# Six orders of products and shifted weight blocks in a two-layer encoder

## Chip, cores and metric

The kernel runs on one core of a Trainium2 chip. The metric is the device time of one execution in microseconds. All inputs and outputs are float32 in HBM.

## What is computed

Two layers of an encoder over 272 tokens (256 and 16 learned ones) of 2048 features. Cut to what matters:

```python
def _layer(h, w_in, ..., w_out, ln1_w, ln1_b, w_ff1, w_ff2, ln2_w, ln2_b):
    proj = jnp.einsum('bld,dp->blp', h, w_in)          # 2048 -> 6176
    y_gla = _gla_mixer(...)                            # gated linear attention, 4 heads
    y_na = _na_mixer(...)                              # neighbourhood attention, 16 heads
    mix = jnp.einsum('blm,md->bld', jnp.concatenate([y_gla, y_na], axis=-1), w_out)
    h = _layer_norm(DEEPNORM_ALPHA * h + mix, ln1_w, ln1_b)
    ff = jnp.einsum('blf,fd->bld', jnp.square(jax.nn.relu(jnp.einsum('bld,df->blf', h, w_ff1))), w_ff2)
    return _layer_norm(DEEPNORM_ALPHA * h + ff, ln2_w, ln2_b)
```

Nearly all of the arithmetic is in the four weight products: w_in, w_out (2048 x 2048), w_ff1 (2048 x 8192) and w_ff2 (8192 x 2048).

## The kernel before, in words

**Products in halves.** TensorE multiplies in a reduced float32 format here, so each operand is split in a high part (a cast) and a low part (the operand less its high part). A product of a weight block W and activations X is then three: high W by high X (called **h** below), high W by low X (**l**), and low W by high X (**w**).

**Weight tiles.** Weights come from HBM as 768 tiles of 128 x 1024, that is eight blocks of 128 x 128 side by side. `made` (L172) issues the transfer into `raw` (L179), ScalarE casts it to `wh` (L180) and VectorE subtracts to `wl` (L181). The pool of these tiles has three buffers for each of raw, wh and wl, and `weights` (L166) makes tiles two ahead of the one in use. `head` (L186) does the same in pieces for the first tile, which arrives together with the first activations. A block of a tile starts 512 bytes after the one before it, in the high and in the low tile, and all these tiles start at multiples of 256 bytes in SBUF.

**Activations.** `pair` (L277) holds the high and low part of 128 features in one tile; a row has a pitch of 288 elements, so the low part lies 1152 bytes behind the high one and the next feature block 2304 bytes behind the first. Some pairs of the second layer are dense (256 and 256 elements).

**Two ways through a tile.** `by_m` (L250) takes one output of 128 features after the other; for each it calls `eight` (L204) once per weight tile, and all products of a call add up in one PSUM bank. `eight` writes out the order: for each of the eight blocks h and then l (L216), then for each of the eight blocks w (L219), so 24 products of up to 274 columns. Where only 256 tokens are needed it takes `once`: high and low activations as one moving operand of 512 columns (L213), eight products, and then eight w products of 256 columns into the second half of the bank (L219), 16 in all. `by_k` (L230) keeps four or eight outputs open at once and has an order of its own (L246).

**Around it.** Between calls `by_m` runs steps of the attention and norm work (`pump`, L121): small products on TensorE, vector work on ScalarE and VectorE. Evictions of finished outputs, casts and subtractions stand in the same queues of ScalarE and VectorE. All weight transfers are issued from SyncE's queue. The place of instructions in each queue is set by a scheduler at build time.

Of the kernel before, what the change touches and what calls it, by code (L numbers as in the profile page):

```python
# [7 lines left out]
F32 = mybir.dt.float32  # L8
F32R = mybir.dt.float32r
U8 = mybir.dt.uint8  # L10
AF = mybir.ActivationFunctionType
ALU = mybir.AluOpType
PSUM = bass.MemoryType.PSUM

P = 128
D = 2048
DC = D // P
T = 256
# [8 lines left out]
WB = 1024  # L27
# [10 lines left out]
MEET = 2  # L38
PAD = 40
PITCH = 288  # L40


class Pair(tuple):
# [10 lines left out]
class Trunk:  # L54
    def __init__(self, ctx, tc, ins, out):
        self.ctx, self.tc, self.nc = ctx, tc, tc.nc
        self.i, self.out = ins, out
        self.bg, self.fg, self.credit, self.fcredit = deque(), deque(), 0, 0
        self.wants, self.due, self.late = {}, None, 0
        self.x = [None] * DC  # L60
        self.stream, self.ready = self.order(), deque()
        pool = lambda name, **k: ctx.enter_context(tc.tile_pool(name=name, **k))
        self.cp = pool("const", bufs=1)
        self.xp = pool("xhl", bufs=1)
        self.yp = pool("yhl", bufs=1)
        self.wp = pool("wst", bufs=3)
        self.jp = pool("jn", bufs=1)
        self.pm = pool("pm", bufs=4, space=PSUM)
        self.pb = pool("pb", bufs=4, space=PSUM)
# [96 lines left out]
    def weights(self):  # L166

        while len(self.ready) < 2:
            self.ready.append(self.made(*next(self.stream, (None, ()))))
        return self.ready.popleft()  # L170

    def made(self, ap, ends):  # L172
        if ap is None:
            return None
        nc = self.nc
        raw, wh, wl = (self.wp.tile([P, WB], d, name=nm, tag=nm)
                       for nm, d in (("raw", F32), ("wh", F32R), ("wl", F32R)))
        for c in map(slice, (0,) + ends, ends):
            nc.sync.dma_start(raw[:, c], ap[:, c])  # L179
            nc.scalar.copy(wh[:, c], raw[:, c])  # L180
            self.wl = nc.vector.tensor_tensor(wl[:, c], raw[:, c], wh[:, c].bitcast(F32), ALU.subtract).ins  # L181
        if not ends:
            self.head(ap, raw, wh, wl)
        return wh, wl

    def head(self, ap, raw, wh, wl):  # L186

        nc, q = self.nc, WB // 4
        both = self.xr.tile([P, 2, q + L], F32, name="head", tag="head", bufs=1)
        self.x[:2] = [self.pair(self.xp, "x", c) for c in range(2)]  # L190
        for c in range(2):
            nc.sync.dma_start(both[:, c], self.i["head"][:, c])
        nc.sync.dma_start(raw[:, 2 * q:], ap[:, 2 * q:])
        for c in range(2):
            at = slice(c * q, c * q + q)
            h, lo = (t[:, :L] for t in self.x[c])
            todo = [(both[:, c, q:], h, lo), (both[:, c, :q], wh[:, at], wl[:, at])]
            for args in todo[::-1] if c else todo:
                self.split(*args)
        for at in (slice(2 * q, 3 * q), slice(3 * q, WB)):  # L200
            nc.scalar.copy(wh[:, at], raw[:, at])
            self.wl = nc.vector.tensor_tensor(wl[:, at], raw[:, at], wh[:, at].bitcast(F32), ALU.subtract).ins

    def eight(self, ps, wh, wl, x, n, first, last, once):  # L204

        mm = self.nc.tensor.matmul
        c = lambda w, j: w[:, j * P:j * P + P]  # L210
        for j, v in enumerate(x):
            if once:
                mm(ps, lhsT=c(wh, j), rhs=v.once, start=first and not j, stop=False)  # L213
                continue
            for i in range(2):
                mm(ps[:, :n], lhsT=c(wh, j), rhs=v[i][:, :n], start=first and not i + j, stop=False)  # L216
        o = ps[:, T:] if once else ps[:, :n]
        for j, (h, _) in enumerate(x):
            mm(o, lhsT=c(wl, j), rhs=h[:, :T if once else n], start=False, stop=last and j == 7)  # L219

    def whole(self, parts):

# [7 lines left out]
    def by_k(self, acts, n, before, wide=False):  # L230

        ps = [self.pm.tile([P, 512], F32, name="mm", tag="mm") for _ in range(4)]
        if wide:
            ps += [self.bank() for _ in range(4)]
        nk = len(acts)
        for k in range(0, nk, 2):
            before(k)
            for g in range(0, len(ps), 4):
                wh, wl = self.weights()
                parts = ((wh, 0), (wh, 1), (wl, 0))  # L240
                order = [(j, p, m) for j in range(2) for p in range(3) for m in range(4)]
                by_output = k == nk - 2 or k == 0 and not wide
                order.sort(key=lambda o: (o[0], o[2] // 2) if wide and not k + g else (by_output and o[2], o[1] // 2))
                for j, p, m in order:
                    c = j * 512 + m * P
                    self.nc.tensor.matmul(ps[g + m][:, :n], lhsT=parts[p][0][:, c:c + P], rhs=acts[k + j][parts[p][1]][:, :n],  # L246
                                          start=k + j + p == 0, stop=k == nk - 2 and j + p == 3)
        return [p[:, :n] for p in ps]

# [27 lines left out]
    def pair(self, pool, name, c):  # L277
        both = pool.tile([P, 2, PITCH], F32R, name=f"{name}{c}", tag=f"{name}{c}", bufs=1)
        return Pair(both, dense=name in ("y", "u") and not self.full)
# [94 lines left out]
    def load_gates(self):  # L374

        place = lambda c: self.yp.tile([P, 2, PITCH], F32, name=f"gw{c}", tag=f"y{c}", bufs=1).rearrange("p a c -> p (a c)")[:, :512]
        *self.wup, self.wlr = (place(c) for c in (8, 9, 10))
# [563 lines left out]
    def reuse(self, name, c, dtype):  # L941

        t = self.xp.tile([P, 2, PITCH], dtype, name=f"{name}{c}", tag=f"x{c}", bufs=1)
        return t.rearrange("p a c -> p (a c)")[:, :512]
# [235 lines left out]
```

## Time and profile before

| | |
|---|---|
| time, median of 3 runs (lowest to highest) | 2366.43 us (2366.19 to 2366.48) |
| the profiled execution's own time | 2366.29 us |
| its span, first to last instruction | 2364.5 us |
| mean granted TensorE clock | 0.999 |
| products of `eight` and `by_k` in the busy table | L216, L219, L213, L246 |
| HBM traffic over the span | 176 GB/s |

The page of the profile gives busy time by engine, the span in 40 slices, DMA queues, the chain of work that ended last, and groups of instructions. A group's line reads: source line, engine, operation, output and inputs by name, shapes, count; then busy time and the mean duration of one in ns; then idle time of the engine just before them and what ended it. PE stands for TensorE's products, PEld for its weight loads, which overlap them; DVE is VectorE, ACT is ScalarE. In the timeline a row merges a run of like instructions: start in us, extent in us, engine, line, names, shapes, and the number merged. A product's shape is rows x columns of the weight block and then the moving operand.

### The profile page before, as it was taken

Reading aid. Unit: us, or ns where it says so; the run is one execution under the profiler, and the core shown is the slowest. Engines: PE = TensorE matmul, PEld = TensorE weight load, DVE = VectorE, ACT = ScalarE, POOL = GpSimd, SP = SyncE. Lnnn points to the kernel's source line nnn. Section 1 sums busy time; section 2 is a strip of 40 time slices with the busy share of each in tenths; the row PEclk is TensorE's granted clock in tenths of the full one; section 3 lists DMA queues with packets and bytes.
Section 4 is the critical chain, followed back from the end, with each engine's and each line's share of the span. In section 5 each row is a group of like instructions: output and inputs, shape, how many; then the busy total and the mean of one; then the engine's idle time right before and its main releaser. Section 6 shows DMA issues by size and latency. Waiting matters only on the chain.

```text
span 2364.5 us, 44607 instructions
## 1 busy us (share of the span) xinstructions
PE 2356.2 (100%) x18180; PEld 2241.9 (95%) x18180; DVE 1520.8 (64%) x2432; ACT 1219.3 (52%) x2100; POOL 136.2 (6%) x200
## 2 busy tenths in 40 slices
PE   9999999999999999999999999999999999999998
PEld 9999999999999999999999899999988888888888
DVE  5588777775544455546576787778766455666654
ACT  5666664564433344444456666655644333444443
POOL 0021100100000000000030111101100000000000
PEclk9999999999999999999999999999999999999999
DMA  7454445555555555555555555455566666556664
GB/s 261 153 160 153 156 135 176 173 176 178 177 178 176 176 177 179 177 177 174 177 184 171 164 160 165 155 160 188 187 192 190 189 187 188 188 190 212 195 188 144
DMA packets 118301, 419.02 MB, mean 177 GB/s; under 512 B 13512, under 2 KB 14024, under 8 KB 118096
## 3 DMA queue, kind: packets, MB, share of 16 engines
q1 hardware_dynamic: 117808, 415.65, 55.8%
q8 instruction: 142, 2.33, 0.4%
q14 instruction: 63, 0.52, 0.1%
q10 hardware_dynamic: 288, 0.52, 0.1%
HBM read 414.03 MB, written 2.10 MB: 176 GB/s over the span
## 4 chain that ended last, share of the span: by engine, by line
PE 98%; DVE 1%; issue 0%; ACT 0%; POOL 0%; DVEq 0%; ACTq 0%; POOLq 0%
PE mm L216 35%; PE mm L219 29%; PE mm L213 22%; PE mm L246 6%; PE bg L246 1%; PE bg L757 1%; PE mm L696 1%; PE bg L557 0%; PE bg L403 0%; DVE wl L181 0%; PE mm L722 0%; PE mm L446 0%; PE bg L883 0%; PE bg L608 0%; PE bg L638 0%
## 5 line engine op out<-in xcount | busy, mean ns | idle before, releaser
L181 DVE TENSOR_TENSOR wl<-raw,wh 128x1024 fp32r<-128x1024 f32 (+1 forms) x768 | 941.8, 1227 | 621.5 <-ACT wh L180 618.4
L180 ACT CAST wh<-raw 128x1024 fp32r<-128x1024 f32 (+1 forms) x768 | 803.5, 1047 | 919.4 <-PE mm L216 367.7
L216 PE MATMUL mm<-x,wh 128*128 128x272 f32 (+2 forms) x4224 | 569.8, 287 | 0.0
L216 PEld LDWEIGHTS mm<-x,wh 128*128 128x128 f32 x4224 | 541.1, 188 | 0.8 <-PE mm L696 0.2
L219 PE MATMUL mm<-x,wl 128*128 128x272 f32 (+3 forms) x3264 | 466.9, 285 | 0.0
L219 PEld LDWEIGHTS mm<-x,wl 128*128 128x128 f32 x3264 | 437.5, 189 | 11.6
L213 PE MATMUL mm<-x,wh 128*128 128x512 f32 x1152 | 290.1, 394 | 0.0
L213 PEld LDWEIGHTS mm<-x,wh 128*128 128x128 f32 x1152 | 207.2, 189 | 37.9 <-PE mm L696 0.4
L219 PE MATMUL mm<-y,wl 128*128 128x272 f32 (+1 forms) x1408 | 200.5, 285 | 0.0
L219 PEld LDWEIGHTS mm<-y,wl 128*128 128x128 f32 x1408 | 189.5, 189 | 6.5
L216 PE MATMUL mm<-y,wh 128*128 128x272 f32 (+1 forms) x1440 | 193.3, 286 | 0.0
L216 PEld LDWEIGHTS mm<-y,wh 128*128 128x128 f32 x1440 | 184.3, 188 | 0.0
L213 PE MATMUL mm<-y,wh 128*128 128x512 f32 x688 | 172.6, 392 | 0.0
L219 PE MATMUL mm<-u,wl 128*128 128x272 f32 (+1 forms) x1024 | 145.8, 285 | 0.0
L213 PEld LDWEIGHTS mm<-y,wh 128*128 128x128 f32 x688 | 123.6, 189 | 21.9
L219 PEld LDWEIGHTS mm<-u,wl 128*128 128x128 f32 x1024 | 137.8, 189 | 4.8
L216 PE MATMUL mm<-u,wh 128*128 128x272 f32 (+1 forms) x1056 | 141.2, 286 | 0.0
L216 PEld LDWEIGHTS mm<-u,wh 128*128 128x128 f32 x1056 | 134.9, 188 | 0.0
L213 PE MATMUL mm<-u,wh 128*128 128x512 f32 x496 | 124.2, 392 | 0.0
L213 PEld LDWEIGHTS mm<-u,wh 128*128 128x128 f32 x496 | 89.2, 189 | 15.9
L246 PE MATMUL mm<-x,wh 128*128 128x272 f32 (+1 forms) x512 | 73.3, 288 | 0.0
L246 PEld LDWEIGHTS mm<-x,wh 128*128 128x128 f32 x512 | 67.9, 191 | 0.0
(273 smaller groups left out, 1856.5 us busy)
## 6 DMA issues: line engine op xcount, KB each, us to landing
raw<-in_wff SPq DMA_DIRECT2D x512, 512.0 KB, 3.6
raw<-in_win SPq DMA_DIRECT2D x190, 512.0 KB, 3.8
raw<-in_wout SPq DMA_DIRECT2D x64, 512.0 KB, 3.6
nb<-in_nab SPq DMA_DIRECT2D x16, 352.0 KB, 4.7
xraw<-in_xT SPq DMA_DIRECT2D x7, 272.0 KB, 5.2
out<-out SPq DMA_DIRECT2D x5, 256.0 KB, 3.2
brow<-in_norm SPq DMA_DIRECT2D x4, 256.0 KB, 4.8
gw<-in_wup SPq DMA_DIRECT2D x4, 196.0 KB
```

The lines of the kernel that those rows point to most:

```text
L180: nc.scalar.copy(wh[:, c], raw[:, c])
L181: self.wl = nc.vector.tensor_tensor(wl[:, c], raw[:, c], wh[:, c].bitcast(F32), ALU.subtract).ins
L213: mm(ps, lhsT=c(wh, j), rhs=v.once, start=first and not j, stop=False)
L216: mm(ps[:, :n], lhsT=c(wh, j), rhs=v[i][:, :n], start=first and not i + j, stop=False)
L219: mm(o, lhsT=c(wl, j), rhs=h[:, :T if once else n], start=False, stop=last and j == 7)
L246: self.nc.tensor.matmul(ps[g + m][:, :n], lhsT=parts[p][0][:, c:c + P], rhs=acts[k + j][parts[p][1]][:, :n], start=k + j + p == 0, stop=k ...
L696: nc.tensor.matmul(ps[hh][:, t * NKEY:t * NKEY + NKEY], lhsT=q[hs, NM + t * P:NM + t * P + P], rhs=k[hs, t, :], start=True, stop=True)
L757: nc.tensor.matmul(po[t][hs, :P], lhsT=v2[ts, hs] if rest else v1[:, t, hs], rhs=p2[ts, hh, :] if rest else p1[:, 2 * hh + t, :], start=re ...
```

## The change

Each pair of consecutive weight tiles draws four things from a fixed hash of its number: the step between blocks of the high tile, the step between blocks of the low tile (128 elements and 0, 16, 32 or 48 more), the offset of the first low block (0, 16, 32 or 48 elements), and one of six orders of the products of a call. In an order each letter is the next product of its kind; where the moving operand is 512 wide, the letters l are left out. The tiles grow from 1024 to 1472 elements, and the space comes from a scratch area for DMA descriptors, which is cut from 8192 to 2048 bytes per partition. `by_k` draws steps and offset too, and keeps its order. The cast and the subtraction now write eight blocks with a step.

```diff
+SKEWS = (0, 16, 32, 48)
+TURNS = ("hlhlhlhlhlhlhlhl wwwwwwww", "hlw hlw hlw hlw hlw hlw hlw hlw", "hlhlww hlhlww hlhlww hlhlww",
+         "hhhhhhhh llllllll wwwwwwww", "hhll hhll hhll hhll wwwwwwww", "hlhlhlhlwwww hlhlhlhlwwww")
+SPAN = 1472
...
-        raw, wh, wl = (self.wp.tile([P, WB], d, name=nm, tag=nm)
-                       for nm, d in (("raw", F32), ("wh", F32R), ("wl", F32R)))
+        raw = self.wp.tile([P, WB], F32, name="raw", tag="raw")
+        blocks = raw.rearrange("p (b c) -> p b c", c=P)
+        a, b, base, turn = self.draw()
+        wh, wl = self.skewed("wh", a, 0), self.skewed("wl", b, base)
         for c in map(slice, (0,) + ends, ends):
             nc.sync.dma_start(raw[:, c], ap[:, c])
-            nc.scalar.copy(wh[:, c], raw[:, c])
-            self.wl = nc.vector.tensor_tensor(wl[:, c], raw[:, c], wh[:, c].bitcast(F32), ALU.subtract).ins
+            self.halves(blocks, wh, wl, slice(c.start // P, c.stop // P))
...
+    def draw(self):
+
+        r = self.tiles // 2 * 2654435761 % 2 ** 32 >> 12
+        self.tiles += 1
+        return SKEWS[r % 4], SKEWS[r // 4 % 4], SKEWS[r // 16 % 4], TURNS[r // 64 % len(TURNS)]
+
+    def skewed(self, name, skew, base):
+        flat = self.wp.tile([P, SPAN], F32R, name=name, tag=name)
+        return bass.AP(flat.tensor, flat.offset + base, [flat.ap[0], [P + skew, WB // P], [1, P]])
+
+    def halves(self, raw, wh, wl, at):
+        self.nc.scalar.copy(wh[:, at], raw[:, at])
+        self.wl = self.nc.vector.tensor_tensor(wl[:, at], raw[:, at], wh[:, at].bitcast(F32), ALU.subtract).ins
...
-        c = lambda w, j: w[:, j * P:j * P + P]
-        for j, v in enumerate(x):
+        c = lambda w, j: w[:, j]
+        seen = dict.fromkeys("hlw", 0)
+        todo = [k for k in self.turn if k in ("hw" if once else "hlw")]
+        for i, kind in enumerate(todo):
+            j = seen[kind]
+            seen[kind] += 1
+            w, v, o = wl if kind == "w" else wh, x[j], ps[:, :n]
+            rhs = v[kind == "l"][:, :n]
             if once:
-                mm(ps, lhsT=c(wh, j), rhs=v.once, start=first and not j, stop=False)
-                continue
-            for i in range(2):
-                mm(ps[:, :n], lhsT=c(wh, j), rhs=v[i][:, :n], start=first and not i + j, stop=False)
-        o = ps[:, T:] if once else ps[:, :n]
-        for j, (h, _) in enumerate(x):
-            mm(o, lhsT=c(wl, j), rhs=h[:, :T if once else n], start=False, stop=last and j == 7)
+                rhs, o = (v.once, ps) if kind == "h" else (v[0][:, :T], ps[:, T:])
+            mm(o, lhsT=c(w, j), rhs=rhs, start=first and not i, stop=last and i == len(todo) - 1)
...
-    nc = bacc.Bacc("TRN2", target_bir_lowering=False, num_devices=1, dynamic_dma_scratch_size=8192)
+    nc = bacc.Bacc("TRN2", target_bir_lowering=False, num_devices=1, dynamic_dma_scratch_size=2048)
```

More of the change, by code (lines that the diff above doesn't have):

```diff
@@ L60, in __init__ @@
         self.x = [None] * DC
-        self.stream, self.ready = self.order(), deque()
+        self.stream, self.ready, self.tiles, self.turns = self.order(), deque(), 0, deque()
         pool = lambda name, **k: ctx.enter_context(tc.tile_pool(name=name, **k))
@@ L169, in weights @@
             self.ready.append(self.made(*next(self.stream, (None, ()))))
+        self.turn = self.turns.popleft()
         return self.ready.popleft()
@@ L173, in made, with head @@
         if ap is None:
+            self.turns.append(None)
             return None
         nc = self.nc
-        raw, wh, wl = (self.wp.tile([P, WB], d, name=nm, tag=nm)
-                       for nm, d in (("raw", F32), ("wh", F32R), ("wl", F32R)))
+        raw = self.wp.tile([P, WB], F32, name="raw", tag="raw")
+        blocks = raw.rearrange("p (b c) -> p b c", c=P)
+        a, b, base, turn = self.draw()
+        wh, wl = self.skewed("wh", a, 0), self.skewed("wl", b, base)
         for c in map(slice, (0,) + ends, ends):
             nc.sync.dma_start(raw[:, c], ap[:, c])
-            nc.scalar.copy(wh[:, c], raw[:, c])
-            self.wl = nc.vector.tensor_tensor(wl[:, c], raw[:, c], wh[:, c].bitcast(F32), ALU.subtract).ins
+            self.halves(blocks, wh, wl, slice(c.start // P, c.stop // P))
         if not ends:
-            self.head(ap, raw, wh, wl)
+            self.head(ap, raw, blocks, wh, wl)
+        self.turns.append(turn)
         return wh, wl
-    def head(self, ap, raw, wh, wl):
+    def draw(self):
[8 more added lines that the diff above has]
+        self.wl = self.nc.vector.tensor_tensor(wl[:, at], raw[:, at], wh[:, at].bitcast(F32), ALU.subtract).ins
+    def head(self, ap, raw, blocks, wh, wl):
         nc, q = self.nc, WB // 4
@@ L194, in head @@
         for c in range(2):
-            at = slice(c * q, c * q + q)
+            at = slice(2 * c, 2 * c + 2)
             h, lo = (t[:, :L] for t in self.x[c])
-            todo = [(both[:, c, q:], h, lo), (both[:, c, :q], wh[:, at], wl[:, at])]
+            todo = [(both[:, c, q:], h, lo), (both[:, c, :q].rearrange("p (b c) -> p b c", c=P), wh[:, at], wl[:, at])]
             for args in todo[::-1] if c else todo:
                 self.split(*args)
-        for at in (slice(2 * q, 3 * q), slice(3 * q, WB)):
-            nc.scalar.copy(wh[:, at], raw[:, at])
-            self.wl = nc.vector.tensor_tensor(wl[:, at], raw[:, at], wh[:, at].bitcast(F32), ALU.subtract).ins
+        for at in (slice(4, 6), slice(6, 8)):
+            self.halves(blocks, wh, wl, at)
     def eight(self, ps, wh, wl, x, n, first, last, once):
         mm = self.nc.tensor.matmul
-        c = lambda w, j: w[:, j * P:j * P + P]
-        for j, v in enumerate(x):
-            if once:
-                mm(ps, lhsT=c(wh, j), rhs=v.once, start=first and not j, stop=False)
-                continue
-            for i in range(2):
-                mm(ps[:, :n], lhsT=c(wh, j), rhs=v[i][:, :n], start=first and not i + j, stop=False)
-        o = ps[:, T:] if once else ps[:, :n]
-        for j, (h, _) in enumerate(x):
-            mm(o, lhsT=c(wl, j), rhs=h[:, :T if once else n], start=False, stop=last and j == 7)
+        c = lambda w, j: w[:, j]
[6 more added lines that the diff above has]
+            rhs = v[kind == "l"][:, :n]
+            if once:
+                rhs, o = (v.once, ps) if kind == "h" else (v[0][:, :T], ps[:, T:])
+            mm(o, lhsT=c(w, j), rhs=rhs, start=first and not i, stop=last and i == len(todo) - 1)
     def whole(self, parts):
@@ L244, in by_k @@
                 for j, p, m in order:
-                    c = j * 512 + m * P
-                    self.nc.tensor.matmul(ps[g + m][:, :n], lhsT=parts[p][0][:, c:c + P], rhs=acts[k + j][parts[p][1]][:, :n],
+                    self.nc.tensor.matmul(ps[g + m][:, :n], lhsT=parts[p][0][:, 4 * j + m], rhs=acts[k + j][parts[p][1]][:, :n],
                                           start=k + j + p == 0, stop=k == nk - 2 and j + p == 3)
```

## The prediction

> **What bounds the kernel now.** I read the page first: the busy line of each engine, the row of the granted clock, then the shares of the chain that ended last.
>
> ```profile
> span 2364.5 us, 44607 instructions
> ...
> PE 2356.2 (100%) x18180; PEld 2241.9 (95%) x18180; DVE 1520.8 (64%) x2432; ACT 1219.3 (52%) x2100; POOL 136.2 (6%) x200
> ...
> PEclk9999999999999999999999999999999999999999
> ...
> PE 98%; DVE 1%; issue 0%; ACT 0%; POOL 0%; DVEq 0%; ACTq 0%; POOLq 0%
> ```
>
> TensorE never waits, its clock is never throttled, and 98% of the chain is its own work. So the time is the sum of the steps from one product to the next, and an edit that leaves the number of products alone can act in two ways only: by the length of a step, or by making TensorE wait where it does not wait today. The groups give the counts, and the two costly feeders:
>
> ```profile
> L181 DVE TENSOR_TENSOR wl<-raw,wh 128x1024 fp32r<-128x1024 f32 (+1 forms) x768 | 941.8, 1227 | 621.5 <-ACT wh L180 618.4
> L180 ACT CAST wh<-raw 128x1024 fp32r<-128x1024 f32 (+1 forms) x768 | 803.5, 1047 | 919.4 <-PE mm L216 367.7
> L216 PE MATMUL mm<-x,wh 128*128 128x272 f32 (+2 forms) x4224 | 569.8, 287 | 0.0
> ...
> L213 PE MATMUL mm<-x,wh 128*128 128x512 f32 x1152 | 290.1, 394 | 0.0
> ...
> L216 PE MATMUL mm<-y,wh 128*128 128x272 f32 (+1 forms) x1440 | 193.3, 286 | 0.0
> L213 PE MATMUL mm<-y,wh 128*128 128x512 f32 x688 | 172.6, 392 | 0.0
> ...
> L216 PE MATMUL mm<-u,wh 128*128 128x272 f32 (+1 forms) x1056 | 141.2, 286 | 0.0
> ...
> L213 PE MATMUL mm<-u,wh 128*128 128x512 f32 x496 | 124.2, 392 | 0.0
> ```
>
> The mean of one (287 ns) is a latency; neighbours overlap, so it is not the price of a product. L216 issues 16 products a tile: 4224 + 1440 + 1056 = 6720, that is 420 **narrow tiles** of 24 products (nearly all 272 wide). L213 issues 8: 1152 + 688 + 496 = 2336, that is 292 **wide tiles** of eight 512-wide and eight 256-wide products. The price is in TensorE's timeline, from one row's start to the next. First narrow tiles, then (two further windows that cut into the run at 401.70) single products, then a wide tile and its second half:
>
> ```profile
> 399.72 2.14 PE L216 MATMUL mm<-y,wh 128*128 128x272 f32 x16
> 401.70 1.16 PE L219 MATMUL mm<-y,wl 128*128 128x272 f32 x8
> 402.70 2.14 PE L216 MATMUL mm<-y,wh 128*128 128x272 f32 x16
> 404.68 1.16 PE L219 MATMUL mm<-y,wl 128*128 128x272 f32 x8
> 405.68 0.54 PE L216 MATMUL mm<-y,wh 128*128 128x272 f32 x3
> ```
>
> ```profile
> 401.82 1.04 PE L219 MATMUL mm<-y,wl 128*128 128x272 f32 x7
> ```
>
> ```profile
> 401.95 0.91 PE L219 MATMUL mm<-y,wl 128*128 128x272 f32 x6
> ```
>
> ```profile
> 1900.92 2.00 PE L213 MATMUL mm<-u,wh 128*128 128x512 f32 x8
> 1902.76 1.12 PE L219 MATMUL mm<-u,wl 128*128 128x256 f32 x8
> 1903.71 2.00 PE L213 MATMUL mm<-y,wh 128*128 128x512 f32 x8
> ```
>
> ```profile
> 1901.85 1.07 PE L213 MATMUL mm<-u,wh 128*128 128x512 f32 x4
> ```
>
> A narrow tile takes 402.70 - 399.72 = 2.98 us, 124.2 ns a product: 123.8 in the high run, 125.0 in the low run. Within one run the steps differ: 0.12 us from 401.70, then 0.13 us, and the six that follow take 0.75 us (125). A wide tile takes 2.79 us; its 512-wide run starts slowly (four in 0.93 us, 232.5 ns each) and settles (four in 0.91 us, 227.5 each); its 256-wide run takes 0.95 us, 118.8 each. So a product of the same width has no fixed price; something in its place and its neighbours moves it by some per cent, and that is what the change shuffles.
>
> **The change part by part.** Products, loads of weights, casts, subtractions and transfers are as many as before; the two built programs hold the same instructions on every engine, with some casts, subtractions and small vector operations changing places. What remains are five edits.
>
> *Order and steps of blocks, narrow tiles.* No row shows narrow tiles with blocks apart by 576, 640 or 704 bytes. The nearest rows are the products of L246: same width, same tiles, another order and another place for the output. The chain in order of time gives whole stages of them, each piece from its first start to the next piece's:
>
> ```profile
> 357.26 15.23 PE mm L246 x120
> ...
> 493.82 24.10 PE mm L246 x192
> ...
> 1679.72 23.04 PE mm L246 x192
> ```
>
> 192 products of 272 columns in 24.10 us are 125.5 ns each; the 120 at 357.26 took 126.9. The 256-wide ones at 1679.72 took 120.0 each, the lowest that a long run shows. So the ends are 120 (-4.2 ns) and 130 (+5.8, the worst step above), that is -42 and +58 us over 420 x 24 products. I take the nearest row: +1.3 ns, 24 x 1.3 = 0.031 us a tile, **+13.0 us** over 420 tiles. I apply it to all six orders, the first (today's) too, since it also gets new steps.
>
> *Steps of blocks, wide tiles.* The nearest row is a wide tile whose moving operand lies in two pieces, in another place to its weights:
>
> ```profile
> 1499.69 2.02 PE L213 MATMUL mm<-x,wh 128*128 128x512 f32 x8
> 1501.55 1.11 PE L219 MATMUL mm<-x,wl 128*128 128x256 f32 x8
> 1502.49 2.17 PE L216 MATMUL mm<-x,wh 128*128 128x272 f32 x16
> ```
>
> Its 512-wide run takes 1.86 us and does not settle (232.5 each); the tile takes 2.80 us instead of 2.79. Ends: 227.5 and 232.5 in all eight instead of 230, -0.02 and +0.02 us a tile. I take +0.01 x 292 = **+2.9 us**.
>
> *Order, wide tiles.* L213's tiles have no l products. Three of the six orders are then today's (144 of the 292 tiles). The order hlw becomes hw eight times (52 tiles): at the settled prices 8 x (227.5 + 118.8) = 2.77 us, -0.02 each, **-1.0 us**. hlhlww and the two half runs (96 tiles) start a high run again and again: 8 x (232.5 + 118.8) = 2.81 us, +0.02 each, **+1.9 us**.
>
> *Stepped writes of the cast and the subtraction.* The trace has such writes: ws, 512 elements in 16 blocks, beside the plain 512-element cast of L180 (the 620 in the row of all casts).
>
> ```profile
> L268 ACT CAST ws<-gw x2: 622/622/623, 27.6 to 1253.9; 128x512 fp32r<-128x512 f32 x2
> L269 DVE TENSOR_TENSOR ws<-gw,ws x2: 686/686/687, 39.1 to 1260.8; 128x512 fp32r<-128x512 f32 x2
> ```
>
> ```profile
> L180 ACT CAST wh<-raw x768: 620/1048/1062, 6.8 to 2341.9; 128x1024 fp32r<-128x1024 f32 x191, 128x512 fp32r<-128x512 f32 x1
> ```
>
> 622 against 620 ns: I count nothing; bounds 0 and 2 ns x 768 on engines that are 52 and 64% busy.
>
> *Later release, earlier want.* In the three orders that mix w among the others, the high tile is read until close to the end instead of until product 16 of 24. The cast into that buffer waits for it (367.7 us of its idle time ends on L216), behind it on ScalarE wait evictions and copies, behind the subtraction on VectorE the layer norm's sums. And the low block is wanted at the third product. The buffers are three and the tiles are made two ahead, so this is covered except where VectorE is full. Two stages by window, then the subtraction and the tile that uses it:
>
> ```profile
> 1230.00:1250.00 20.00, 20.00 (x161) 20.00 (x160) 18.90 (x32) 13.56 (x26) 11.70 (x6) 1.00 0.59 185
> ...
> 1575.00:1600.00 25.00, 25.00 (x145) 21.98 (x144) 24.56 (x56) 14.92 (x27) 0.00 (x0) 1.00 0.50 167
> ```
>
> ```profile
> 1578.43 1.22 DVE L181 TENSOR_TENSOR wl<-raw,wh 128x1024 fp32r<-128x1024 f32 x1
> ```
>
> ```profile
> 1579.29 2.00 PE L213 MATMUL mm<-y,wh 128*128 128x512 f32 x8
> 1581.13 1.11 PE L219 MATMUL mm<-y,wl 128*128 128x256 f32 x8
> ```
>
> The low block is ready at 1579.65. Today it is wanted at 1581.13; in the order hw it is wanted at 1579.29 + 0.23 = 1579.52, 0.13 us too early. With one order in six so early, and about 15 tiles in these 45 us of the span, I count 0 and keep 5.3 us as the other end: the high tile is released at product 23, 22 or 20, so 7, 6 or 4 steps of 124 ns later, 0.70 us on the mean, in half of 15 tiles.
>
> *Places and scratch.* The smaller scratch pays for the wider tiles and moves all tiles down alike, by 6144 bytes. The page's queues are all of the hardware kind and a tile lands 3.6 us after its issue; I count 0.
>
> ```profile
> raw<-in_wff SPq DMA_DIRECT2D x512, 512.0 KB, 3.6
> ```
>
> **The sum**, against the profiled execution's own time, 2366.3 us (its span 2364.5 and 1.8 around it; the median of the runs is 2366.4): 2366.3 + 13.0 + 2.9 - 1.0 + 1.9 = **2383.1, forecast 2383 us**, +0.7%.
>
> **The rivals.** *Order and place do not matter (2366).* Then a step depends on width alone, and the differences inside a run average out over any order; no term of the sum is left. For it: a whole narrow tile takes 2.98 us again and again, and the 256-wide products take 120.0 in L246's order and 118.8 in L219's. Against it: 124.2 and 125.5 for the same 272 columns, 227.5 and 232.5 for the same 512. [...]
>
> *The draws settle better than today's order (faster).* The mechanism: after a change of run the steps are long (232.5, 130) and then fall (227.5). Orders that repeat every two or three products may settle once and stay. Place: all narrow tiles. Price: if the mean step falls halfway to the floor of 120.0, 2.1 ns x 24 x 420 = 21 us, and 0.02 x 292 = 6 us in the wide tiles, 2339 us in full, some 2352 for half of that. It decides as soon as the mean narrow step lies below 124.2. Against it: the one other order that the trace has, L246's, also repeats and takes more.
>
> *Both more collisions and late weights (much slower).* At L246's worst stage, 126.9, the narrow tiles cost 2.7 x 24 x 420 = 27 us; with 3.8 for the wide ones and 5.3 for late weights, 2403 us.
>
> That the change does less than it says: L246's products and those 144 wide tiles keep their order; the sum counts it so.
>
> **How the numbers follow.** Forecast 0.53; order and place without effect 0.17; faster 0.16; much slower 0.14. A measurement of this kernel tells about 0.2%, 4.7 us, from no change: slower 0.53 + 0.14 = 0.67, same 0.17, faster 0.16. The range runs from 2356, which takes in the smaller half of the faster case, to 2400, which leaves out the upper half of the worst: about 0.15 outside.
>
> **What would show it.** In the changed timeline, narrow tiles of the order that is still hlhl… then w at 3.0 us against 2.98, others between 2.98 and 3.05; wide tiles in hw at 2.77. TensorE still 100% busy. Wrong if narrow tiles average 2.98 or less, if TensorE shows idle time ended by the subtraction, or if the casts or subtractions take longer than 1048 and 1228 ns.

## The result, and the profile after

The changed kernel takes 2375.8 us (five runs, 2375.28 to 2376.43) against 2366.43 before (2365.74 to 2366.82): a ratio of 1.004 with a 95% interval of 1.0026 to 1.0055, or +9.4 us. The forecast was 2383, the range 2356 to 2400. The page of the changed kernel, the lines that answer to those of before:

```profile
span 2373.5 us, 44595 instructions
...
PE 2366.2 (100%) x18180; PEld 2248.0 (95%) x18180; DVE 1524.0 (64%) x2432; ACT 1217.6 (51%) x2100; POOL 135.5 (6%) x200
...
PEclk9999999999999999999999999999999999999999
...
PE 99%; DVE 0%; ACT 0%; DVEq 0%; issue 0%
...
L206 DVE TENSOR_TENSOR wl<-raw,wh 128x1024 fp32r<-128x1024 f32 (+1 forms) x770 | 942.3, 1224 | 651.7 <-ACT wh L205 642.1
L205 ACT CAST wh<-raw 128x1024 fp32r<-128x1024 f32 (+1 forms) x770 | 804.6, 1046 | 912.3 <-PE mm L241 656.9
```

The span is 9.0 us longer and TensorE is busy 10.0 us more with the same 18180 products, at the same granted clock (0.999 in both). Casts and subtractions take what they took (1046 and 1224 ns against 1047 and 1227). The view of waits on TensorE has one line (three, together 2.2 us, in the kernel before):

```profile
PE bg L393 <- DVE zero L390: 1.2, 1, 1.2
```

That is the start of the kernel. So the whole loss is in the steps between products. The timeline shows them tile by tile: first a narrow tile in today's order whose low tile only is shifted by 64 bytes, then two tiles in the order hhhhhhhh llllllll wwwwwwww, with the blocks of both halves 704 bytes apart and an offset of 192 bytes.

```profile
416.45 2.15 PE L241 MATMUL mm<-y,wh 128*128 128x272 f32 x16
418.44 1.15 PE L241 MATMUL mm<-y,wl 128*128 128x272 f32 x8
419.43 0.41 PE L241 MATMUL mm<-y,wh 128*128 128x272 f32 x2
```

```profile
428.40 2.19 PE L241 MATMUL mm<-y,wh 128*128 128x272 f32 x16
430.42 1.18 PE L241 MATMUL mm<-y,wl 128*128 128x272 f32 x8
431.43 2.19 PE L241 MATMUL mm<-y,wh 128*128 128x272 f32 x16
433.45 1.18 PE L241 MATMUL mm<-y,wl 128*128 128x272 f32 x8
434.46 0.29 PE L241 MATMUL mm<-y,wh 128*128 128x272 f32 x1
```

2.98 us for the first, 3.03 for each of the others. Not every draw loses. A wide tile with low blocks 640 bytes apart and 64 bytes of offset takes 2.75 us where every tile took 2.79 before:

```profile
1900.88 2.00 PE L241 MATMUL mm<-y,wh 128*128 128x512 f32 x8
1902.72 1.08 PE L241 MATMUL mm<-y,wl 128*128 128x256 f32 x8
1903.63 2.00 PE L241 MATMUL mm<-y,wh 128*128 128x512 f32 x8
1905.47 1.08 PE L241 MATMUL mm<-y,wl 128*128 128x256 f32 x8
1906.38 0.40 PE L241 MATMUL mm<-u,wh 128*128 128x512 f32 x1
```

Its eight high products take 1.84 us as before, its eight low ones 0.91 instead of 0.95. Summing the steps from start to start over both traces, the 376 tiles with 272 columns lose 10.1 us and the 292 wide ones 0.6; L246's products (L267 in the changed kernel) gain 0.9, the remaining narrow tiles 0.2 and all other small products 0.5. Among tiles whose products stand back to back, only 11 of 325 narrow ones take today's 2.980 us or less, against 84 of 278 wide ones below today's 2.793.

### The profile page after: what moved, and what is told of

It reads as the page before. It is cut to its first block, busy times and chain, and to the rows that moved or that the text cites. A ratio compares the mean times of both kernels' runs of the same rounds, so it can differ in the third digit from the quotient of the medians.

```text
span 2373.5 us, 44595 instructions
## 1 busy us (share of the span) xinstructions
PE 2366.2 (100%) x18180; PEld 2248.0 (95%) x18180; DVE 1524.0 (64%) x2432; ACT 1217.6 (51%) x2100; POOL 135.5 (6%) x200
## 4 chain that ended last, share of the span: by engine, by line
PE 99%; DVE 0%; ACT 0%; DVEq 0%; issue 0%
PE mm L241 88%; PE mm L267 6%; PE bg L267 1%; PE bg L778 1%; PE mm L717 1%; PE bg L578 1%; PE bg L424 0%; PE mm L743 0%; PE mm L467 0%; PE bg L904 0%; PE bg L629 0%; PE bg L659 0%; PE bg L661 0%; PE bg L660 0%; PE bg L633 0%; PE bg L393 0%
## 5 line engine op out<-in xcount | busy, mean ns | idle before, releaser
L206 DVE TENSOR_TENSOR wl<-raw,wh 128x1024 fp32r<-128x1024 f32 (+1 forms) x770 | 942.3, 1224 | 651.7 <-ACT wh L205 642.1
L205 ACT CAST wh<-raw 128x1024 fp32r<-128x1024 f32 (+1 forms) x770 | 804.6, 1046 | 912.3 <-PE mm L241 656.9
L241 PE MATMUL mm<-x,wh 128*128 128x272 f32 (+3 forms) x5376 | 966.4, 311 | 0.0
L241 PE MATMUL mm<-x,wl 128*128 128x272 f32 (+3 forms) x3264 | 586.0, 285 | 0.0
L241 PEld LDWEIGHTS mm<-x,wl 128*128 128x128 f32 x3264 | 492.1, 188 | 20.6
L241 PE MATMUL mm<-y,wh 128*128 128x272 f32 (+2 forms) x2128 | 414.8, 322 | 0.0
L241 PE MATMUL mm<-u,wh 128*128 128x272 f32 (+2 forms) x1552 | 299.7, 322 | 0.0
L241 PE MATMUL mm<-y,wl 128*128 128x272 f32 (+1 forms) x1408 | 256.2, 284 | 0.0
L241 PE MATMUL mm<-u,wl 128*128 128x272 f32 (+1 forms) x1024 | 183.8, 284 | 0.0
L267 PE MATMUL mm<-x,wh 128*128 128x272 f32 (+1 forms) x512 | 72.7, 287 | 0.0
L267 PEld LDWEIGHTS mm<-x,wh 128*128 128x128 f32 x512 | 67.3, 189 | 0.0
L994 POOL TENSOR_SCALAR acc<-acc,vec 128x272 f32<-128x272 f32 (+1 forms) x24 | 45.4, 1896 | 272.6 <-DVE acc L1006 142.9
L555 ACT COPY U<-S 128x272 f32<-128x272 f32 (+1 forms) x104 | 40.9, 428 | 22.4 <-DVE S L564 18.6
L564 DVE TENSOR_TENSOR S<-S,dec 128x272 f32<-128x272 f32 (+1 forms) x112 | 46.4, 442 | 3.9 <-ACT U L555 3.3
```

The costliest lines, as they stand in the source:

```text
L205: self.nc.scalar.copy(wh[:, at], raw[:, at])
L206: self.wl = self.nc.vector.tensor_tensor(wl[:, at], raw[:, at], wh[:, at].bitcast(F32), ALU.subtract).ins
L241: mm(o, lhsT=c(w, j), rhs=rhs, start=first and not i, stop=last and i == len(todo) - 1)
L555: nc.scalar.copy(U[:, lv % 4, j, :w].rearrange("p (n t h) -> p n t h", t=2, h=hb), bass.AP(S.tensor, S.offset + 2 * j * L, [S.ap[0], [2 * ...
L564: tt(o, o, totals(lv, odd, w), ALU.mult)
L994: nc.gpsimd.tensor_scalar(a, a, gain, bias, ALU.mult, ALU.add)
```

## The experiments

The theories, as they stood after the result. **Pattern**: a step's length is a fixed function of a tile's order and places together; today's narrow tile is a good pattern, and nearly any other costs a little more. Its rivals: only the **order** matters, only the **places** matter, or **late weights** hold TensorE up. All kernels below start from the changed one unless it is said otherwise; their before is the same kernel on the same chip, 2366.4 to 2366.6 us.

**e1_place and e2_order: one half of the draw each.**

```diff
 # e1_place
-        return SKEWS[r % 4], SKEWS[r // 4 % 4], SKEWS[r // 16 % 4], TURNS[r // 64 % len(TURNS)]
+        return SKEWS[r % 4], SKEWS[r // 4 % 4], SKEWS[r // 16 % 4], TURNS[0]
 # e2_order
+        return 0, 0, 0, TURNS[r // 64 % len(TURNS)]
```

> Steps and offset drawn as in the change, every tile in today's order (h, l alternating, then w). Theory pattern (the length of a step is a fixed function of order and place together; today's narrow tile of 2.98 us is a good one and nearly any other costs about 0.02 to 0.03 us more): 2372 to 2376 us. Theory order (only the sequence of kinds matters): 2366 to 2367. Theory place (only the places of the blocks matter): the whole 2376. Theory late weights: 2366, since the high tile is released as early as before.

> Orders drawn as in the change, blocks 512 bytes apart as before. Theory pattern: 2370 to 2376 us, and with the run of the places alone the two parts add up to more than the change's 9.4 us. Theory order: the whole 2376. Theory place: 2366. Theory late weights: about 2376, with idle time of TensorE ended by the subtraction.

Measured: places alone 2374.82 us, ratio 1.0034 (1.0021 to 1.0047), +8.2 us; order alone 2372.57, ratio 1.0025 (1.0016 to 1.0035), +6.0 us. Each half alone costs most of the whole, which fells the theories of order alone and of place alone. 8.2 + 6.0 is also more than 9.4. The totals alone do not settle that, since their intervals are wide, but the steps do: the 376 tiles with 272 columns lose 7.7 us by places, 5.0 by orders and 10.1 by both, where the same sum agrees within 0.1 us between the kernel before, e3_layout and e9_all below. The parts do not add up. TensorE waits for no weights in e2_order (its view of waits has the same single line), which fells late weights. (In e4_pick, e7_blocks and e8_draws below it waits for a subtraction once each, for 0.5 to 0.6 us.)

**e3_layout: neither half.** `return 0, 0, 0, TURNS[0]`: wider tiles, small scratch and moved places stay.

> Neither drawn: today's order, blocks 512 bytes apart; what is left is the wider tiles, the smaller scratch and the moved places of all tiles. Pattern, order and place: 2366 us, narrow tiles at 2.98, wide ones at 2.79. If scratch or layout is the cause: up to 2376.

Measured: 2366.31 us, ratio 0.9998 (0.999 to 1.0007). Scratch and layout cost nothing that shows against 2366.4 to 2366.6. Its blocks lie side by side again, so it does not test the stepped writes; that these cost nothing is shown by the changed kernel's own 1046 and 1224 ns. This kernel also gives the yardstick for whole stages, since all its products stand in one line. In the chain in order of time (start, extent, count of products) its two longest pieces are a stretch of narrow and a stretch of wide tiles:

```profile
517.48 551.81 PE mm L241 x4444
...
1702.30 517.46 PE mm L241 x2963
```

The same two pieces in the changed kernel, then in e1_place and in e2_order:

```profile
520.15 556.98 PE mm L241 x4444
...
1710.77 518.19 PE mm L241 x2963
```

```profile
520.34 555.85 PE mm L241 x4444
...
1710.34 518.55 PE mm L241 x2963
```

```profile
518.86 554.19 PE mm L241 x4444
...
1706.67 518.81 PE mm L241 x2963
```

Per narrow product that is 124.2 ns without draws, 125.3 with all, 125.1 with places and 124.7 with orders. Wide tiles hardly change on the mean.

**e4_pick: the best draws everywhere.** WIDE is the set of the wide tiles' numbers.

```diff
+        return (0, 32, 16, TURNS[0]) if self.tiles - 1 in WIDE else (0, 48, 0, TURNS[2])
```

> No draw: every wide tile has low blocks 640 bytes apart, offset 64 bytes, today's order; every other tile has low blocks 704 bytes apart and the order hlhlww. In the changed kernel's trace tiles with these draws took 2.75 us (wide) and 2.96 us (narrow), against 2.79 and 2.98. Theory pattern: these hold in every tile, 292 x 0.04 + 400 x 0.02 = 20 us less than before, 2345 to 2350 us. If a tile's length hangs on chance or on its neighbours rather than on its own order and place: 2370 to 2380.

Measured: 2351.55 us, ratio 0.9936 (0.9923 to 0.9948), -15.0 us. The median narrow tile of 272 columns takes 2.960 us and the median wide one 2.753, as the two draws had promised; a narrow product takes 547.62 / 4440 = 123.3 ns:

```profile
517.60 547.62 PE mm L242 x4440
...
1697.29 510.06 PE mm L242 x2963
```

It misses the expected 2345 to 2350 by a little. Summed over the steps, the picked tiles are worth 17.2 us against the 20 worked out from rounded lengths; the tiles of L246 got the narrow pattern's steps with an order of their own and became 1.9 us slower than in e3_layout; and 1.1 us more went to small products and waits outside the weight products. A tile's time can thus be chosen by its pattern, here with neighbours of the same pattern.

**e7_blocks and e8_draws: orders for themselves, and another sample.** In e7_blocks no place is drawn and sixteen tiles in a row share an order; e8_draws only replaces the hash.

```diff
 # e7_blocks
+        return 0, 0, 0, TURNS[(self.tiles - 1) // 16 % len(TURNS)]
 # e8_draws
+        r = (self.tiles - 1) // 2 * 2246822519 % 2 ** 32 >> 11
```

> No steps; sixteen tiles in a row have the same order, then the next sixteen the next, so each of the six has settled rows of its own. Theory pattern: each order has a narrow tile of its own that repeats to the nanosecond, one of them 2.98 (today's), the others 2.98 to 3.03; 2366 to 2376 us. Theory neighbours (the cost of the drawn orders is the change of order from tile to tile): each order settles at 2.98.

> The change with another hash: another sample of the same draws. Theory pattern: the sum of some 350 draws changes little, 2373 to 2379 us, and where a draw of the change comes back the tile takes the same time as there. If the change's draws were unlucky as a whole: back to 2366.

Measured, one run each: 2375.44 and 2379.65 us; the second is 0.65 above the expected ceiling of 2379. The tiles of 272 columns lose 10.2 us in e8_draws against 10.1 in the change, so that part came back; what its trace has more than the change's is 0.9 us in the wide tiles, 1.7 in L246's and 1.9 outside the weight products. In e7_blocks the narrow tiles settle by order. Today's order, the high run in all h then all l, and the order hhll:

```profile
664.28 2.14 PE L241 MATMUL mm<-y,wh 128*128 128x272 f32 x16
666.26 1.16 PE L241 MATMUL mm<-y,wl 128*128 128x272 f32 x8
667.26 0.41 PE L241 MATMUL mm<-y,wh 128*128 128x272 f32 x2
```

```profile
807.81 2.18 PE L241 MATMUL mm<-y,wh 128*128 128x272 f32 x16
809.83 1.16 PE L241 MATMUL mm<-y,wl 128*128 128x272 f32 x8
810.83 0.41 PE L241 MATMUL mm<-y,wh 128*128 128x272 f32 x2
```

```profile
855.92 2.17 PE L241 MATMUL mm<-x,wh 128*128 128x272 f32 x16
857.92 1.16 PE L241 MATMUL mm<-x,wl 128*128 128x272 f32 x8
858.92 0.29 PE L241 MATMUL mm<-x,wh 128*128 128x272 f32 x1
```

2.98, 3.02 and 3.00 us by the rows (tiles of the second order take 3.013 to 3.020 in the trace); the three mixed orders all settle at 2.987. Without drawn places today's order is the best of the six for 272 columns. The loss does not come from changing the order between tiles: it is 5.4 us in the 376 tiles here, 5.0 in e2_order. The low runs are 1.00 us in all three: the difference is in the high run. For wide tiles, hw settles at 2.773 in one stretch and at 2.820 to 2.831 in two others, hhww at 2.787, and the half runs at 2.807. The stretches of hw read other activations; and in the two slow ones every third tile takes 2.820 and the rest 2.830, while the tiles rotate through three buffers. So order and step of the blocks alone do not fix a tile's time; which of the differences between the stretches counts, no run separates. In e8_draws a draw that the change also had takes the same time again; a wide tile with low blocks 576 bytes apart and an offset of 192, first in the changed kernel and then in e8_draws:

```profile
1970.80 1.99 PE L241 MATMUL mm<-y,wh 128*128 128x512 f32 x8
1972.62 1.10 PE L241 MATMUL mm<-y,wl 128*128 128x256 f32 x8
1973.56 0.40 PE L241 MATMUL mm<-u,wh 128*128 128x512 f32 x1
```

```profile
1778.85 1.99 PE L242 MATMUL mm<-x,wh 128*128 128x512 f32 x8
1780.67 1.11 PE L242 MATMUL mm<-x,wl 128*128 128x256 f32 x8
1781.62 0.39 PE L242 MATMUL mm<-x,wh 128*128 128x512 f32 x1
```

2.76 and 2.77 us, to the nanosecond 2767 in both, with other activations and other work around. Over the changed kernel, e1_place and e8_draws, take the tiles whose products stand back to back, with another such tile behind them, and whose draw was seen more than once (for wide tiles, orders that are alike without l count as one). Of those that stand second in their pair, 271 of 342 wide ones and 278 of 351 narrow ones (272 columns) lie within 2 ns of their draw's median; of those that stand first, behind a tile of another draw, 207 of 339 and 234 of 369. So most tiles repeat, and the tile before counts too.

**e5_pitch, e6_shift, e9_all: what must stay in place to what.** Two theories: **meeting** (the load of a block runs beside the stream of activations, and their places to each other count) and **loads** (only the step from one loaded block to the next counts). The first and the third start from the kernel before.

```diff
 # e5_pitch (of before), with dynamic_dma_scratch_size=2048
-PITCH = 288
+PITCH = 304
 # e6_shift, with return 0, 0, 16, TURNS[0]
-        wh, wl = self.skewed("wh", a, 0), self.skewed("wl", b, base)
+        wh, wl = self.skewed("wh", a, 16), self.skewed("wl", b, base)
 # e9_all (of before)
-PAD = 40
+PAD = 56
```

> The kernel before with a row pitch of the activations of 304 instead of 288 elements (the low part 1216 bytes behind the high one, the next feature block 2432) and the small scratch; weight blocks, order and everything else as before. Theory meeting (a step's length comes from how the load of the next block and the stream of the moving operand meet, so their places to each other count): narrow tiles leave 2.98 us for some 3.00 to 3.02, 2370 to 2378 us. Theory loads (only the step from one loaded block to the next counts): narrow 2.98, wide 2.79, 2366 us.

> Both the high and the low tile start 64 bytes later, blocks 512 bytes apart, today's order: the weights are shifted against the activations and the step between blocks is not. Theory meeting: another pattern, most likely 3.00 to 3.02 us for a narrow tile, 2370 to 2378 us. Theory loads: 2366 us, 2.98 and 2.79.

> The kernel before with the pad at the bottom of SBUF 64 bytes longer, so that weight tiles and activations all start 64 bytes later and keep their places to each other. Theory meeting (their places to each other count): 2.98 us for a narrow and 2.79 for a wide tile, 2366 us. If the place of a weight block itself counts (where it starts within 128 or 256 bytes): as in the run that shifted the weights alone, 3.00 and 2.77.

Measured: e5_pitch 2371.13 us (ratio 1.002, 1.0011 to 1.003), e6_shift 2364.82 (0.9993, 0.9984 to 1.0002), e9_all 2366.88 (1.0003, 0.9993 to 1.0012). In e6_shift, whose weights lie 64 bytes off against the activations with every step between blocks as before, the two long pieces, a narrow tile and a loop of L246 (here L267) are:

```profile
519.92 555.51 PE mm L241 x4444
...
1706.74 513.75 PE mm L241 x2963
```

```profile
401.51 2.17 PE L241 MATMUL mm<-y,wh 128*128 128x272 f32 x16
403.52 1.16 PE L241 MATMUL mm<-y,wl 128*128 128x272 f32 x8
404.51 1.67 PE L241 MATMUL mm<-y,wh 128*128 128x272 f32 x12
```

```profile
1684.97 21.77 PE mm L267 x192
```

A narrow tile takes 3.00 us instead of 2.98, the stretch of wide ones 3.7 us less than in e3_layout, and the last line, 192 products of 256 columns with several outputs open, 21.77 us instead of 23.04: 113.4 ns each instead of 120.0. The total hides it: e6_shift missed the expected 2370 to 2378 because gains of 5.1 us in the wide tiles and 2.8 in L246's ate the 7.6 lost in the 376 narrow ones. e5_pitch moves the activations instead, against the weights and against each other; in its timeline a narrow tile takes 3.02 us (401.46 to 404.48), and wide ones 2.79 and 2.80 (from 1899.61 to 1902.40 and on to 1905.20). e9_all moves both together, and nothing changes: 2.98 and 2.79, and its 192 products again take

```profile
1680.46 23.04 PE mm L246 x192
```

So loads falls, and what meeting says of the places holds: those of weights and activations to each other count. A shift of 64 bytes of the weights against the activations is worth 6.6 ns in 120 here (113.4 against 120.0); what in the chip makes it so, no run shows. Nor is it shown that the length of a load matters. In the kernel before, a run of small products beside the weight tiles streams 272 columns against weight blocks of only 64 or 32 columns, in other places, whose loads take 135 and 108 ns on the mean where those of the weight tiles take 188 to 191; 32 of these products take 3.98 us, 124.4 ns each:

```profile
56.50 4.15 PE L403 MATMUL bg<-x,ws 128*64 128x272 f32 x32
60.48 0.29 PE L216 MATMUL mm<-x,wh 128*128 128x272 f32 x1
```

**e10_pick2: a place for the last tiles too.** MANY is the set of the tiles of `by_k`; the fifth value is the offset of the high tile.

```diff
+        if self.tiles - 1 in MANY:
+            return 0, 0, 16, TURNS[0], 16
+        return (0, 32, 16, TURNS[0], 0) if self.tiles - 1 in WIDE else (0, 48, 0, TURNS[2], 0)
```

> As the run that picked places and orders, but the tiles of the loops with several open outputs take blocks 512 bytes apart, both tiles shifted by 64 bytes (in the run that shifted everything these took 2.98 us, and 2.72 where they are 256 wide, against 3.03 and 2.86 in the first pick). Theory pattern: 40 x 0.05 + 16 x 0.13 = 4 us less than the first pick, 2347 us. If such tiles' lengths do not carry over: 2352.

Measured: 2347.25 us, ratio 0.992 (0.9907 to 0.9934), 19.1 us less than before and 28.5 less than the change. The 192 products took 21.79 us. It is the fastest kernel of this study.

## Why the prediction was right, step by step

- *What bounds the kernel.* Right: TensorE stayed at 100%, waits did not grow, and the loss is in the steps. ("TensorE never waits" leaves out 2.2 us.)
- *Order and steps of blocks, narrow tiles, +13.0 us.* Right in mechanism, a little too large: +10.1 us in the 376 tiles of 272 columns and -0.2 in the others. The price taken from the rows of L246, +1.3 ns a product, measured 556.98 / 4444 - 551.81 / 4444 = 1.2 ns in the long stretch. That it came so near is luck in part: L246's rows are one pattern among many, and nothing made them the mean of the draws. The lower end of 120 ns was read off products of 256 columns and carried to 272; the 118.8 that the prediction itself read in the wide tiles lies below it. Charging today's order too was right: with places alone it loses as well (e1_place).
- *Steps of blocks, wide tiles, +2.9, and their orders, -1.0 and +1.9.* This term was mis-sized: +0.6 us in all instead of +3.8. The row for the steps, a moving operand in two pieces, is one pattern of many, and drawn places also give patterns that settle low (2.75). Of the orders, the half runs came out as worked out (2.807 against 2.81); hw settles at 2.773, as worked out, in one stretch and at 2.82 to 2.83 in two; hhww is 2.787 where 2.81 was forecast.
- *L246's products, no change taken.* They draw places too and gained 0.9 us, hardly more than they vary without draws (0.4 less than before in e3_layout, 0.7 more in e9_all).
- *Stepped writes, 0; scratch and layout, 0.* Right: 1046 and 1224 ns for the writes, and e3_layout at 2366.31 us for the rest.
- *Late weights, 0.* Right: no wait of TensorE for a subtraction in the changed kernel.
- *Rival: order and place do not matter.* It falls with e1_place and e2_order, and e6_shift shows it most plainly. The reading that 120.0 is a floor for 256 columns, on which its support partly stood, falls too: it was 120.0 in the places of before and 113.4 in e6_shift.
- *Rival: the draws settle better.* It did not come on the mean, yet single draws settle below today's tile (2.75 us against 2.79 for a wide one), and chosen ones take 19.1 us off. The settling itself came out unevenly: with no places drawn hlw settles at 2.987, above today's 2.980, and hw at 2.773 in one stretch and 2.82 to 2.83 in two (e7_blocks). What it missed is that random draws bring the average draw, and today's narrow tile is better than that (11 of 325 drawn ones reach it).
- The sum counted order and places as one price per product, not as two to be added. The experiments show that this was needed: the 376 tiles lose 7.7 and 5.0 us alone, 10.1 together.

## What to carry to other kernels

Here TensorE was 100% busy with 2.2 us of waits, and the steps from product to product inside one tile were still uneven (227.5 to 232.5 ns for 512 columns). Where another trace shows products of one shape in unequal steps, their order and the places of weights against activations can be tried like any other setting, by drawing many in one run and reading each tile's time from the trace. Choose per kind of tile, and judge each kind by itself: the one shift of e6_shift gained 5.1 us in the wide tiles and lost 7.6 in the narrow ones. The mean over random draws said nothing about the best here, 9.4 us lost against 19.1 gained by chosen ones, and the effects of places and orders measured alone did not add up (7.7 and 5.0 us in the 376 tiles, 10.1 together).

## What the runs showed that was not expected

- The lowest steps of two widths are alike by the column: products of 256 columns go down to 113.3 ns (the mean of seven in a row in the changed kernel; 113.4 over the 192 of e6_shift) and those of 512 to 226.7 (the last three of a settled run in before), 0.443 ns a column in both; 272 columns would then take 120.4, an estimate from these two widths that no trace reaches over a run of twelve (the lowest mean of twelve such steps in a row, in any of them, is 122.2). By this estimate the pattern's price is 124.2 - 120.4 = 3.8 ns a narrow product before, 4.9 in the change, 2.9 in the pick.
- The 256-wide products of before settled at 120.0 ns in both loops of L246 that have them, and looked like a limit of their own. Moving the weights by 64 bytes took it away (113.4 in e6_shift).
- Most drawn patterns repeat within 2 ns across three kernels (271 of 342 wide and 278 of 351 narrow tiles that stand second in their pair), with other data, other activations and other work on VectorE and ScalarE; nothing here points to traffic of other engines as the cause of the uneven steps, though no run took that traffic away.
